# A block with a convolution and gated attention: the sigmoids of gates that are read back get a fixed place in ScalarE's queue

## The chip, the cores and the metric

The kernel runs on one core of a Trainium2 chip. The metric is the device time of one execution in microseconds (us); what is compared is the median of several runs. A profile of one execution is there too, with its own time. PE is TensorE (matmuls; PEld is its weight load), DVE is VectorE, ACT is ScalarE, POOL is GpSimd, SP is SyncE, which here only issues DMAs. Each engine works through a queue of its own in order; semaphores hold an instruction until what it needs is there.

## The reference, cut to what matters

For one sequence of 512 tokens of width 1024, the block is a half-weighted SwiGLU, a mixer, a second half-weighted SwiGLU and a norm. The change lies in the mixer:

```python
z = h @ w_in
cb, cc, cu, q, k, v, g_lr, r, ga, gb = jnp.split(z, SPLIT_POINTS, axis=-1)
y_conv = (cb * causal_short_conv(cc * cu, conv_w)) @ w_out_conv
...                                   # o: gated linear attention of q, k, v, g_lr, 4 heads
o = o * lax.rsqrt(jnp.mean(o * o, axis=-1, keepdims=True) + EPS)
y_gla = (o * gla_norm_g * jax.nn.silu(r)) @ w_out_gla
merged = jax.nn.sigmoid(ga) * y_conv + jax.nn.sigmoid(gb) * y_gla
return merged @ w_o
```

`ga` and `gb` are two gates of 512 x 1024. Each multiplies one product.

## The kernel before, in words

All arithmetic is float32, made from a rounded part and a rest: a weight tile `f` (128x1024) is cast on ACT to a high part `wh` (L309), and DVE subtracts to get the low part `wl` (L310). Three matmuls stand for one: high by high, high by low, low by high. There are three buffers each of `wh` and `wl`, so the cast of a step waits until PE is through with the step three places back. Weight tiles are loaded by SP (L283, ten buffers `f`) in the order of a list `STEPS`; `W.take` hands out the next pair and issues casts two steps ahead.

Most products are done as sets of seven products on half matrices (named m1, p2, q6, p5, q7, p4, p3, all run by `Set.run`, whose matmuls are L501, 24 of 256 columns in a step). Sums of weight tiles for them are made by accumulating DMAs from POOL (L287, `f<-f`) and on DVE (L296). Sums of results go through `tp` tiles (six buffers in the mixer); L506 copies a bank to one. Between the steps, hooks of `run_sets` place the parts of the attention: for head 3, `output(3)` (L1150 to L1159) and then `squares(3)`, in which ACT casts the sums of squares (L388), DVE subtracts (L389), PE sums over partitions with a matrix of ones (L1165 for the high part, L1166 for the low) and DVE turns the result (L1167).

The raw gates are made early, among the sets of `w_in`, and are stored in DRAM by ACT's queue (L1324, `ga<-tp` and `gb<-tp`), since there is no room for them. After the sets of `w_in` (the last are those of `r`, with a Silu on ACT, L1317) comes the product with `w_out_conv`: eight output blocks `d` of 128 rows, each one weight tile and 24 matmuls of 512 columns (`mm_single`, lines L337, L338, L339). Block `d` is multiplied by the sigmoid of block `d` of `ga`. In the same loop half a block of `gb` is read for later, into tiles that are free by then: the four `v` tiles for d below 4, the tiles `g` (E, M, KS, EX) after that. The product with `w_out_gla` follows as two sets of seven, with the operands cast in L549 and subtracted in L550.

A helper `gate` reads a block back by SP and applies the sigmoid on ACT, in place:

```python
t = T() if t is None else t
nc.sync.dma_start(t, gates_d[name][d])          # L1368; L1370 for a half block of two
nc.scalar.activation(t, t, AF.Sigmoid)          # L1372
```

The order of each engine's queue isn't the order of the source: a scheduler places each instruction in its engine's queue by what it expects to be ready. So an instruction that stands late in the source can come early in a queue. ACT functions come in tables; where the next function is in another table, an ACT_TABLE_LOAD stands in the queue.

Of the kernel before, what the change touches and what calls it, by code (L numbers as in the profile page):

```python
# [11 lines left out]
AF = mybir.ActivationFunctionType  # L12
# [6 lines left out]
KD = D // P  # L19
# [47 lines left out]
def unit_cols(u):  # L67
    return u[2] * len(u[3]) * u[4]
# [115 lines left out]
def block_kernel(ctx: ExitStack, tc: tile.TileContext, xT, vecs, gf, gup, wgl, wts, out):  # L184
    nc = tc.nc
# [20 lines left out]
    def tile_of(pool, shape, dtype=F32):  # L206
        cnt[0] += 1
        return pools[pool].tile(shape, dtype, tag=pool, name=f"{pool}{cnt[0]}")

    def T(dtype=F32):  # L210
        return tile_of("tp", [P, S], dtype)
# [31 lines left out]
    class Weights:  # L243
# [45 lines left out]
        def issue(self):  # L289
            at = self.issued  # L290
            self.fetch(at)
            for n in self.loads.get(at, ()):
                self.raw[n] = [self.dma(n + i) for i in range(4)] + [tile_of("f", [P, 1024])]
            for n in self.sums.get(at, ()):
                a11, a12, a21, a22, s3 = self.raw[n]
                nc.vector.tensor_tensor(out=s3, in0=a11, in1=a21, op=ALU.add)  # L296
                self.add(a21, a22)
            n, p = STEPS[at]
            w = unit_cols(PLAN[n])
            if p is None:  # L300
                raw = self.raw[n]
            else:
                a11, a12, a21, a22, s3 = self.raw[n]
                raw = {"m1": a11, "p2": a12, "q6": a11, "p5": a21, "q7": s3, "p4": a22,
                       "p3": a12}[p]
            late = at >= len(STEPS) - TAIL or ENDS[0] - TAIL <= at < ENDS[0] - 2
            h = tile_of("op" if late else "wh", [P, 1024], F32R)
            l = tile_of("op" if late else "wl", [P, 1024], F32R)
            nc.scalar.copy(h[:, :w], raw[:, :w])  # L309
            nc.vector.tensor_tensor(out=l[:, :w], in0=raw[:, :w], in1=h[:, :w].bitcast(F32),  # L310
                                    op=ALU.subtract)
            if p == "m1":
                self.add(a11, a21)
            if p == "p2":
                self.add(a12, a11)
            self.issued += 1
            self.ready.append((h, l))
# [10 lines left out]
    W = Weights(2)  # L328
# [12 lines left out]
    def mm_single(mat, kt, col, ah, al):  # L341
        o = MM()
        for u in single(mat, kt, col):
            h, l = W.take(u)
            for i in range(u[2]):
                k = u[1] + i
                mm3(o, h[:, i * P : (i + 1) * P], l[:, i * P : (i + 1) * P],
                    ah[k], al[k], k == 0, k == kt - 1)
        return o
# [124 lines left out]
    def mul(out_, a, b, eng=None):  # L474
        (eng or nc.vector).tensor_tensor(out=out_, in0=a, in1=b, op=ALU.mult)
# [449 lines left out]
    def mixer(norm, nxt):  # L925
# [301 lines left out]
        def pair(t):  # L1227
            return t.rearrange("p (e t) -> p e t", t=HW)

        def half(l):  # L1230
            return slice(l * HW, (l + 1) * HW)
# [128 lines left out]
        def parts(v):  # L1360
            r = [hl for i in v for hl in split_pair(i)]
            return [a for a, _ in r], [b for _, b in r]

        def gate(name, d, l=None, t=None):

            t = T() if t is None else t
            if l is None:
                nc.sync.dma_start(t, gates_d[name][d])  # L1368
            else:
                nc.sync.dma_start(pair(t), gates_d[name][d : d + 2, :, half(l)].rearrange(  # L1370
                    "e p t -> p e t"))
            nc.scalar.activation(t, t, AF.Sigmoid)  # L1372
            return t

        c_h, c_l = parts([Y[i][:, :, 2:] for i in range(4)])
        m = [two(d // 2)[:, d % 2] for d in range(KD)]
# [7 lines left out]
        AT = {3: "m1", 4: "p2", 6: "p5"}  # L1384
        gb = {}

        def early_gate(i, a, l, t):
            gb[i, a, l] = gate("gb", 4 * i + 2 * a, l, t)

        for d in range(KD):  # L1390
            t = gate("ga", d)
            yp = mm_single("w_out_conv", KD, d * P, c_h, c_l)
            mul(m[d], yp, t)
            if d < HEADS:
                tr, orow = (E, M) if d % 2 else (KS, QS)
                nc.vector.tensor_copy(
                    tr.rearrange("p (b c) -> p b c", c=32),
                    r64[:, 16 * d : 16 * (d + 1)].unsqueeze(2).to_broadcast([P, 16, 32]))
                nc.vector.transpose(orow, tr)
                mul(O[d], O[d], orow.unsqueeze(1).to_broadcast([P, 2, S]))  # L1400
            if d in AT:
                oo.make(AT[d])
            if d < 4:
                early_gate(0, d % 2, d // 2, vt[1][d])
            else:
                early_gate(1, d % 2, (d - 4) // 2, (E, M, KS, EX)[d - 4])
        oo.sum("q6")
        m_h, m_l = [None] * KD, [None] * KD

        def gla_done(i):  # L1410
# [56 lines left out]
    with phase("small2", f=10, tp=6, v=4, qk=2, g=1, y=4, small=1):  # L1467
        W.phase(4, 5)
        n2 = Norm(V_G2)
        mixer(nm, n2)  # L1470
# [46 lines left out]
```

## Time and profile before

| | |
|---|---|
| runs | 1196.65, 1197.68, 1200.97 us; median 1197.68 |
| profiled execution | 1196.36 us, of which the span from the first to the last instruction is 1194.6 us; 1.76 us lie around it |
| PE | 1179.0 us busy, 99% of the span |
| DVE, ACT, POOL | 74%, 53%, 10% |
| granted TensorE clock, mean | 0.995 |

In the profile, a time in the first column is that of the start of an instruction, counted from the start of the span; the second is how long it took. `L1372` is line 1372 of the kernel. In square brackets stands how long the engine was idle before the instruction, and what released it. "ACTq" and "SPq" are DMA issues and waits in an engine's queue, which aren't counted as busy. Numbers in buffer names are left out in the profile, and shown in the order of the queues below.

### The profile page before, as it was taken

The numbers are of one execution on the slowest core, as the hardware profiler recorded it, in microseconds if no ns is written. First come the engines' busy times: TensorE is split into PE (matmuls) and PEld (weight loads), VectorE is DVE, ScalarE is ACT, GpSimd is POOL, SyncE is SP. The second block draws the span as 40 slices with busy tenths as digits, with TensorE's granted clock in tenths as the row PEclk, the third lists the DMA queues.
The fourth block names the chain that finished last, engine by engine and source line by source line (L and its number), as shares of the span: only waits on it lengthen the run. The fifth ranks groups of instructions, "written<-read, shape, count | busy, mean of one in ns | idle before, by whom it ended". The sixth has DMA issues, their size and how long they took to land. (4 is left out here: it accounts for less than half of the span.)

```text
span 1194.6 us, 19198 instructions
## 1 busy us (share of the span) xinstructions
PE 1179.0 (99%) x7818; PEld 1086.8 (91%) x7818; DVE 878.7 (74%) x1044; ACT 630.3 (53%) x780; POOL 116.3 (10%) x155
## 2 busy tenths in 40 slices
PE   9999999999999999999989999999999999999997
PEld 8899999988888889999989998998889999998876
DVE  7976666897578765768668778676598665679955
ACT  6564444676245465646545467444346454556543
POOL 0011111111010000101001100200001111101100
PEclk9999999999999999999989999999999999999999
DMA  9477777678532326767867767552528777757721
GB/s 348 85 207 188 179 184 187 157 196 202 194 115 80 94 65 160 218 161 179 221 165 181 189 177 221 160 158 71 185 64 210 177 192 170 184 154 187 175 86 71
DMA packets 61224, 197.10 MB, mean 165 GB/s; under 512 B 6768, under 2 KB 13040, under 8 KB 61136
## 3 DMA queue, kind: packets, MB, share of 16 engines
q0 software_dynamic: 18560, 67.12, 30.6%
q1 hardware_dynamic: 37936, 124.27, 29.7%
q10 hardware_dynamic: 4640, 4.49, 1.2%
q8 instruction: 61, 1.00, 0.3%
q14 instruction: 27, 0.22, 0.1%
HBM read 124.55 MB, written 8.39 MB: 111 GB/s over the span
## 5 line engine op out<-in xcount | busy, mean ns | idle before, releaser
L501 PE MATMUL mm<-op,wh 128*128 128x256 f32 x3584 | 649.8, 284 | 1.5 <-ACT tp L506 1.5
L309 ACT CAST wh<-f 128x1024 fp32r<-128x1024 f32 (+1 forms) x335 | 350.2, 1047 | 436.7 <-PE mm L501 226.0
L501 PEld LDWEIGHTS mm<-op,wh 128*128 128x128 f32 x3584 | 560.4, 192 | 2.6 <-ACT tp L506 1.7
L310 DVE TENSOR_TENSOR wl<-f,wh 128x1024 fp32r<-128x1024 f32 (+1 forms) x335 | 406.9, 1217 | 179.9 <-ACT wh L309 174.9
L501 PE MATMUL mm<-op,wl 128*128 128x256 f32 x1792 | 508.1, 284 | 0.2 <-DVE wl L310 0.2
L501 PEld LDWEIGHTS mm<-op,wl 128*128 128x128 f32 x1792 | 344.1, 192 | 0.6 <-DVE wl L310 0.4
L287 POOL DMA_DIRECT2D f<-f x120 | 103.5, 865 | 927.0 <-DVE wl L310 506.1
L339 PE MATMUL mm<-op,wl 128*128 128x512 f32 x192 | 75.0, 391 | 0.5 <-DVE wl L310 0.5
L337 PE MATMUL mm<-op,wh 128*128 128x512 f32 x192 | 75.2, 392 | 0.2 <-ACT wh L309 0.2
L338 PE MATMUL mm<-op,wh 128*128 128x512 f32 x192 | 74.7, 389 | 0.0
L361 PE MATMUL mm<-op,wh 128*128 128x512 f32 x256 | 64.0, 392 | 0.0
L791 PE MATMUL mm<-wl,op 128*128 128x512 f32 x160 | 62.4, 390 | 0.7 <-DVE wl L310 0.7
L789 PE MATMUL mm<-wh,op 128*128 128x512 f32 x160 | 62.3, 389 | 0.0
L793 PE MATMUL mm<-wh,op 128*128 128x512 f32 x160 | 62.3, 389 | 0.0
L361 PEld LDWEIGHTS mm<-op,wh 128*128 128x128 f32 x256 | 48.0, 189 | 10.2
L506 ACT COPY tp<-mm 128x512 f32<-128x512 f32 x96 | 55.6, 580 | 1.0 <-DVE tp L1299 1.0
L296 DVE TENSOR_TENSOR f<-f,f 128x1024 f32<-128x1024 f32 x40 | 48.9, 1221 | 0.8
L339 PEld LDWEIGHTS mm<-op,wl 128*128 128x128 f32 x192 | 36.0, 188 | 8.4 <-DVE wl L310 1.0
L337 PEld LDWEIGHTS mm<-op,wh 128*128 128x128 f32 x192 | 36.0, 188 | 7.7 <-ACT wh L309 0.4
L338 PEld LDWEIGHTS mm<-op,wh 128*128 128x128 f32 x192 | 36.1, 188 | 7.4
L791 PEld LDWEIGHTS mm<-wl,op 128*128 128x128 f32 x160 | 30.1, 188 | 7.4 <-DVE wl L310 1.3
L793 PEld LDWEIGHTS mm<-wh,op 128*128 128x128 f32 x160 | 30.0, 188 | 6.2
(282 smaller groups left out, 1333.8 us busy)
## 6 DMA issues: line engine op xcount, KB each, us to landing
f<-wts SPq DMA_DIRECT2D x219, 512.0 KB, 4.4
f<-f POOLq DMA_DIRECT2D x120, 512.0 KB, 5.0
X<-xT SPq DMA_DIRECT2D x8, 256.0 KB, 5.2
xs<-X POOLq DMA_DIRECT2D x8, 256.0 KB, 2.3
ga<-tp ACTq DMA_DIRECT2D x8, 256.0 KB, 2.9
gb<-tp ACTq DMA_DIRECT2D x8, 256.0 KB, 3.3
tp<-ga SPq DMA_DIRECT2D x8, 256.0 KB, 5.3
X<-xs POOLq DMA_DIRECT2D x8, 256.0 KB, 6.3
```

The lines of the kernel that those rows point to most:

```text
L287: nc.gpsimd.dma_start(out_, a, accum_op=ALU.add)
L309: nc.scalar.copy(h[:, :w], raw[:, :w])
L310: nc.vector.tensor_tensor(out=l[:, :w], in0=raw[:, :w], in1=h[:, :w].bitcast(F32), op=ALU.subtract)
L337: nc.tensor.matmul(o, wh, ah, start=first, stop=False)
L338: nc.tensor.matmul(o, wh, al, start=False, stop=False)
L339: nc.tensor.matmul(o, wl, ah, start=False, stop=last)
L361: nc.tensor.matmul(o[c], w[:, s : s + P], a[k], start=k == 0 and j == 0, stop=k == kt - 1 and j == 2)
L501: nc.tensor.matmul(to, ww[:, s], aa[:, t], start=fresh and k == 0 and e == 0 and j == 0, stop=k == 3 and j == 2, skip_group_check=True)
L506: nc.scalar.copy(v, o)
L789: nc.tensor.matmul(o[t], bh[:, s], wh, start=fresh and k == 0, stop=False, skip_group_check=True)
L791: nc.tensor.matmul(o[t], bh[:, s], wl, start=False, stop=False, skip_group_check=True)
L793: nc.tensor.matmul(o[t], bl[:, s], wh, start=False, stop=k == 3, skip_group_check=True)
```

## The change

The sigmoid leaves `gate` and becomes a function of its own, which is traced at the loop of `w_out_conv`. An `issue_after` puts it in ACT's queue behind the weight cast that stands last in the source at that place (`W.cast`). The first two blocks of `ga` are read before the loop, and block d + 2 at step d. The half blocks of `gb` are read where they were in the source; their sigmoids come one loop step later, the last one behind the loop.

```diff
-            nc.scalar.copy(h[:, :w], raw[:, :w])
+            self.cast = nc.scalar.copy(h[:, :w], raw[:, :w]).ins
...
-            nc.scalar.activation(t, t, AF.Sigmoid)
             return t
+
+        def sigmoid(t):
+
+            with tc.issue_after(W.cast):
+                nc.scalar.activation(t, t, AF.Sigmoid)
...
+        ga = [gate("ga", d) for d in range(2)]
+        gb_new = []
+
         def early_gate(i, a, l, t):
             gb[i, a, l] = gate("gb", 4 * i + 2 * a, l, t)
+            gb_new.append(gb[i, a, l])

         for d in range(KD):
-            t = gate("ga", d)
+            t = ga[d]
+            if d + 2 < KD:
+                ga.append(gate("ga", d + 2))
+            sigmoid(t)
+            for g in gb_new:
+                sigmoid(g)
+            gb_new.clear()
             yp = mm_single("w_out_conv", KD, d * P, c_h, c_l)
             mul(m[d], yp, t)
...
         oo.sum("q6")
+        sigmoid(gb_new.pop())
```

What this does to the queues is seen in their order. First, ACT at the end of `output(3)`, in the middle of the sets of `w_in`. `wh` are weight casts, `v` and `g_564` are half blocks of `gb`, `tp_5963` is the high part that L1165 on PE needs, and the DMA stores a piece of the raw gate `gb`. Before:

```order
L1158 ACTIVATE g_563_3763<-aux_5888 128x512
L1372 ACT_TABLE_LOAD
L1372 ACTIVATE g_564_3764<-g_564_3764 128x512
L309 CAST wh_5932<-f_5519 128x1024
L1372 ACTIVATE v_3486<-v_3486 128x512
L1372 ACTIVATE v_3487<-v_3487 128x512
L1372 ACTIVATE v_3488<-v_3488 128x512
L1372 ACTIVATE v_3489<-v_3489 128x512
L388 CAST tp_5963<-g_561_3761 128x512
L1324 DMA gb<-tp_5960 128x2x256
L309 CAST wh_5972<-f_5523 128x1024
```

With the change:

```order
L1158 ACTIVATE g_563_3763<-aux_5888 128x512
L309 CAST wh_5932<-f_5519 128x1024
L309 CAST wh_5972<-f_5523 128x1024
L1324 DMA gb<-tp_5960 128x2x256
L388 CAST tp_5963<-g_561_3761 128x512
L309 CAST wh_6003<-f_5773 128x1024
```

Five sigmoids and a table load have left this place. L388 stands now behind one weight cast more, `wh_5972`, and behind the store. On PE, in the same place, L1165 stood behind ten matmuls of the step that uses `wh_5902`; it stands behind twenty now, and L1166 behind all 24:

```order
L501 MATMUL mm_5815<-op_4289,wh_5902 128x256
L1165 MATMUL aux_5967<-tp_5963,ones_r 128x512
L501 MATMUL mm_5815<-op_4288,wl_5903 128x256
L501 MATMUL mm_5815<-op_4288,wh_5902 128x256
L501 MATMUL mm_5815<-op_4289,wh_5902 128x256
L501 MATMUL mm_5815<-op_4288,wl_5903 128x256
L1166 MATMUL aux_5967<-tp_5964,ones_r 128x512
L501 MATMUL mm_6002<-op_4221,wh_5932 128x256
```

So both matmuls of the ones moved ten and more places back.

The second place is ACT at the end of the last set of `r` and in the first blocks of `w_out_conv`. `wh_7220`, `wh_7253`, `wh_7326` are the casts for blocks 0, 1 and 2. Before:

```order
L1372 ACT_TABLE_LOAD
L1372 ACTIVATE g_561_3761<-g_561_3761 128x512
L506 COPY tp_7178<-mm_6991 128x512
L309 CAST wh_7186<-f_6731 128x1024
L1356 CAST op_7298<-y_3483 128x1024
L1317 ACT_TABLE_LOAD
L1317 ACTIVATE tp_7180<-tp_7180 128x512
L1317 ACTIVATE tp_7215<-tp_7215 128x512
L309 CAST wh_7220<-f_7116 128x1024
L1311 ACTIVATE tp_7249<-mm_6991 128x512
L309 CAST wh_7253<-f_7148 128x1024
```

With the change (`wh_7330` is block 2, `wh_7370` block 3; `tp_7311` and `tp_7313` are blocks 0 and 1 of `ga`):

```order
L506 COPY tp_7178<-mm_6991 128x512
L309 CAST wh_7186<-f_6731 128x1024
L1356 CAST op_7298<-y_3483 128x1024
L1317 ACTIVATE tp_7180<-tp_7180 128x512
L309 CAST wh_7220<-f_7116 128x1024
L1317 ACTIVATE tp_7215<-tp_7215 128x512
L309 CAST wh_7253<-f_7148 128x1024
L1311 ACTIVATE tp_7249<-mm_6991 128x512
```

and, six rows further on (two table loads are among them),

```order
L1377 ACT_TABLE_LOAD
L1377 ACTIVATE tp_7311<-tp_7311 128x512
L1377 ACTIVATE tp_7313<-tp_7313 128x512
L309 CAST wh_7370<-f_7218 128x1024
L1377 ACTIVATE tp_7315<-tp_7315 128x512
L1377 ACTIVATE v_3487<-v_3487 128x512
L549 CAST op_7521<-O 128x1024
L309 CAST wh_7410<-f_7251 128x1024
```

The cast of block 0 moved ahead of the second Silu, and a sigmoid and two table loads ahead of it are gone. From block 3 on, a weight cast stands behind the sigmoid of a block read back, as it did before. On SP the reads of `ga` have moved a little too. Before:

```order
L283 DMA f_7364<-wts 128x1024
L1368 DMA tp_7311<-ga 128x512
L1368 DMA tp_7360<-ga 128x512
L1368 DMA tp_7400<-ga 128x512
L283 DMA f_7404<-wts 128x1024
```

With the change:

```order
L283 DMA f_7368<-wts 128x1024
L283 DMA f_7408<-wts 128x1024
L1368 DMA tp_7311<-ga 128x512
L1368 DMA tp_7313<-ga 128x512
L1368 DMA tp_7315<-ga 128x512
```

The weight tile of the last block of `w_out_conv` goes out ahead of the first read now. The reads of `gb` into `v` tiles stay where they were in SP's queue. POOL's queue is the same, and after `w_out_conv` all queues are.

## The prediction, made before the changed kernel ran

> **What bounds the kernel now.** First the page: how long the span is, and who is busy.
>
> ```profile
> span 1194.6 us, 19198 instructions
> ## 1 busy us (share of the span) xinstructions
> PE 1179.0 (99%) x7818; PEld 1086.8 (91%) x7818; DVE 878.7 (74%) x1044; ACT 630.3 (53%) x780; POOL 116.3 (10%) x155
> ```
>
> PE is busy for 99%. So only what makes PE wait, or slows it, can be won, and a busy microsecond less on ACT is worth nothing by itself. The view of who waited for whom, on PE, names the waits (total us, times, longest); the first row comes from the stretch 585 to 625 us, the other three from 700 to 800 us:
>
> ```profile
> PE aux L1165 <- ACT tp L388: 4.3, 1, 4.3
> ```
> ```profile
> PE mm L501 <- ACT tp L506: 1.5, 1, 1.5
> PE mm L339 <- DVE wl L310: 0.5, 1, 0.5
> PE mm L337 <- ACT wh L309: 0.2, 1, 0.2
> ```
>
> One wait of 4.3 us is the longest by far. It ends with the cast L388 on ACT. The timeline of ACT (start, us, ..., idle before) shows what stood ahead of it:
>
> ```profile
> 591.89 1.28 ACT L1372 ACT_TABLE_LOAD   x1
> 593.19 0.63 ACT L1372 ACTIVATE g<-g 128x512 f32<-128x512 f32 x1
> 593.73 1.03 ACT L309 CAST wh<-f 128x1024 fp32r<-128x1024 f32 x1
> 595.96 0.63 ACT L1372 ACTIVATE v<-v 128x512 f32<-128x512 f32 x1 [1.19 <-DMA v<-gb]
> 597.87 0.63 ACT L1372 ACTIVATE v<-v 128x512 f32<-128x512 f32 x1 [1.28 <-DMA v<-gb]
> 600.01 1.30 ACT L1372 ACTIVATE v<-v 128x512 f32<-128x512 f32 x2 [1.51 <-DMA v<-gb]
> 600.77 0.37 ACTq L1324 DMA_DIRECT2D gb<-tp  x1
> 601.22 0.60 ACT L388 CAST tp<-g 128x512 fp32r<-128x512 f32 x1
> ```
>
> Five sigmoids of `gb`, whose results are not used before the product with `w_out_gla`, were placed here. Three times ACT stands still for a read, and L388 with all that follows stands behind. The timeline of PE in the same stretch:
>
> ```profile
> 596.86 0.28 PE L501 MATMUL mm<-op,wl 128*128 128x256 f32 x1
> 596.98 0.40 PE L501 MATMUL mm<-op,wh 128*128 128x256 f32 x2
> 597.22 0.28 PE L501 MATMUL mm<-op,wl 128*128 128x256 f32 x1
> 597.34 0.28 PE L501 MATMUL mm<-op,wh 128*128 128x256 f32 x1
> 601.87 0.79 PE L1165 MATMUL aux<-tp,ones_r 128*128 128x512 f32 x1 [4.26 <-ACT tp L388]
> 602.47 0.41 PE L501 MATMUL mm<-op,wh 128*128 128x256 f32 x1
> ...
> 606.52 0.48 PE L501 MATMUL mm<-op,wh 128*128 128x256 f32 x2
> ```
>
> Three matmuls start in 0.36 us before the wait (596.86 to 597.22), so 0.12 us each. After it they are slow until 606.52. The table by stretches (PE, PEld, DVE, ACT, POOL, then the granted clock, DMA share, GB/s) says why:
>
> ```profile
> 601.90:606.50 4.60, 4.60 (x19) 4.41 (x20) 2.55 (x4) 1.46 (x2) 0.00 (x0) 0.50 0.12 41
> ```
>
> The clock is granted at half after the pause. The wait costs its idle time and this.
>
> **First term: the stall at 597 us.** The change takes the sigmoids from this place. The next start was due at 597.34 + 0.12 = 597.46; full pace is back at 606.52, 9.06 us later. By the order of the queue, PE did 17 matmuls L501 (four between the two of ones, 13 behind) and L1165 and L1166 in that time. At full pace that is 17 x 0.12 = 2.04 us and, with 0.23 us for one of 512 columns (below), 0.46 us: 2.5 us. The stall costs 9.06 - 2.5 = **6.56 us**, of which 4.3 us are idle.
>
> What is late next? PE's step that holds L1165 began ten matmuls before 597.46, at 596.26; L1165 comes after twenty now, at 598.66, and L1166 at 598.66 + 0.23 + 4 x 0.12 = 599.37. On ACT, the cast `wh_5972` is released by the step that ended at 596.26, and takes 1.03 us: done at about 597.4. The store of `gb` behind it needs a sum on DVE that isn't early:
>
> ```profile
> 596.46 0.69 DVE L1302 TENSOR_TENSOR tp<-mm,tp 128x512 f32<-128x512 f32 x1 [0.44 <-PE mm L501]
> ```
>
> That ends at 597.15, so the issue (0.37) runs to 597.8, and L388 (0.60) to 598.4: 0.2 us ahead of L1165. On DVE the subtract for `wl_5973` stands ahead of L389 now; with 1.22 us (below) it ends at 598.7, and L389, as long as L1302, at 599.4. So L1166 comes at the same time as its operand, and PE may wait 0.1 us. Both ends: if a release costs a few tenths at each of these four handovers, up to 1 us of waiting; if the store should hold L388 to where it is now, all 6.56 us stay (a rival). I take 0.2 us. The five sigmoids themselves (5 x 0.63) land in the loop of `w_out_conv`.
>
> [...]
>
> **Second term: the start of `w_out_conv`.** PE's timeline there:
>
> ```profile
> 718.42 0.28 PE L501 MATMUL mm<-op,wl 128*128 128x256 f32 x1
> 718.85 0.50 PE L337 MATMUL mm<-op,wh 128*128 128x512 f32 x1 [0.15 <-ACT wh L309]
> 719.19 0.40 PE L338 MATMUL mm<-op,wh 128*128 128x512 f32 x1
> 720.11 0.50 PE L339 MATMUL mm<-op,wl 128*128 128x512 f32 x1 [0.53 <-DVE wl L310]
> 720.45 0.40 PE L337 MATMUL mm<-op,wh 128*128 128x512 f32 x1
> 720.68 0.39 PE L338 MATMUL mm<-op,wh 128*128 128x512 f32 x1
> ```
>
> The pace for 512 columns is 0.23 us (720.45 to 720.68). L337 was due at 718.54, the L338 of 720.68 four matmuls later at 719.46. So **1.2 us** are lost, more than the 0.7 us that the waits add up to. The cause is the cast of the first block's weights, late on ACT:
>
> ```profile
> 713.40 1.05 ACT L309 CAST wh<-f 128x1024 fp32r<-128x1024 f32 x1 [1.71 <-DMA f<-f]
> 714.35 1.04 ACT L1356 CAST op<-y 128x1024 fp32r<-128x1024 f32 x1
> 715.41 1.28 ACT L1317 ACT_TABLE_LOAD   x1
> 716.71 1.16 ACT L1317 ACTIVATE tp<-tp 128x512 f32<-128x512 f32 x2
> 717.77 1.03 ACT L309 CAST wh<-f 128x1024 fp32r<-128x1024 f32 x1
> ```
>
> A table load stands between, because the queue has a sigmoid of `gb` among the Silus. With the change the cast at 713.40 still waits for its accumulating DMA, but the table load is gone, and one Silu instead of two is ahead of the next weight cast: it starts at 715.4 + 0.6 = 716.0, 1.8 us sooner, is done at 717.1, and the subtract at about 718.3, just before PE is ready at 718.54.
>
> ```profile
> L310 DVE TENSOR_TENSOR wl<-f,wh 128x1024 fp32r<-128x1024 f32 (+1 forms) x335 | 406.9, 1217 | 179.9 <-ACT wh L309 174.9
> ```
>
> I take the whole 1.2 us; the bounds are none of it (if the subtract comes after another on DVE) and all.
>
> **What costs nothing while it is covered.** The sigmoids go among the eight blocks of `w_out_conv`. A block lasts 24 x 0.23 = 5.4 us of PE; ACT's work for one is a cast (1.03), two sigmoids (1.26) and now and then an operand cast (1.04), so 3.3 us. Block 3's matmuls begin at 718.54 + 3 x 5.4 = 734.9 us; its cast stands behind the reads of `ga` blocks 0 and 1:
>
> ```profile
> 720.46 1.37 SPq L1368 DMA_DIRECT2D tp<-ga  x3
> ```
> ```profile
> DMA to landing us min/median/max: 2.1/4.6/7.5
> ```
>
> SP issues these reads after one weight tile more, whose buffer is free when the subtract for block 1 is done, by the work ahead of it on DVE at about 721.3; so the reads go out at about 721.8, 1.3 us later than now. Landed at the longest 7.5 us later, sigmoid, cast and subtract end at 721.8 + 0.4 + 7.5 + 0.6 + 1.0 + 1.2 = 732.5: 2.4 us of cover is left. Without it each us late is one on PE. The 1.5 us wait at L506, near 798 us, hangs on an accumulating DMA of the last set of `w_out_gla`; nothing ahead of it changes order, so I leave it (bounds: gone, or 1 us longer). DMAs, the arithmetic and the bytes are the same.
>
> **Sum.** 6.56 - 0.2 + 1.2 = 7.6 us off the profiled execution: a span of 1187.0 us, a time of 1188.8 us. The median of the runs stands 1.3 us above the profiled one (1197.68 against 1196.36), so **1190.1 us**. A difference of 0.5% (6.0 us) is about the least that a measurement of this kernel tells from no change: 1191.7 us is that limit, and the forecast is only 1.6 us beyond it.
>
> **Rivals.**
>
> *The stall stays, behind the store.* L388 now stands behind the store of `gb`, which left at 600.77 in the row above. There it stood behind L388 in the queue and went out while the last sigmoid ran, and its sum was ready at 597.15: so it was late by the sigmoids alone, which speaks against this rival. For it speaks that no row shows it in its new place. If it leaves no sooner, L388 ends at 601.8 as before and only 1.2 us are won: 1196.5 us. If it's held half as long, about 1193.
>
> *The cover in `w_out_conv` is thinner than it looks.* Two operand casts wait there for sums on DVE, and a weight cast stands behind each. If the second term isn't won and one wait of a us or two, short enough to leave the clock, comes in: -6.4 + 1 to 2, so 1192.3 to 1193.3 us.
>
> *Slower: a weight cast caught behind a late read.* Behind the sigmoid of a block stands the cast of a later block's weights. It decides when a read takes 9.9 us from issue to landing (7.5 + 2.4), where 7.5 is the longest seen; then PE waits, and after a pause like that at 597 us it runs at half clock. Priced as two such stalls (2 x 6.56 = 13.1 us): -7.6 + 13.1 = +5.5, 1203.2 us. Against it: before, sigmoids stood ahead of the same casts, and ACT waited for reads of `ga` for 1.0 us in all (700 to 770 us):
>
> ```profile
> ACT tp L1372 <- DMA tp<-ga: 1.0, 3, 0.4
> ```
>
> *It doesn't do what it says.* The queues show the sigmoids moved, so only a stall that other work causes at the same place could keep the time: 1197.7 us.
>
> **How the numbers follow.** The forecast 0.64, with its own range 1188 to 1192 us; the store 0.13; thinner cover 0.15; slower 0.05; nothing 0.03. The forecast lies beyond the limit for nine parts in ten (0.58), thinner cover for a fifth (0.03): faster 0.61. The store, the rest of those two and nothing at all are within 0.5%: 0.34. Slower: 0.05. The range goes from 1187.5 (without the L506 wait 1188.6, and less where the new median stands nearer to its fastest runs) to 1196.5 us, the store's case; above it lie the slower case and nothing, below it little.
>
> **What would show it.** First term: PE's wait L1165 <- L388 is gone or under 0.5 us, and the granted clock is 1.00 from 597 to 607 us. A wait of L1165 that remains with the store's issue late on ACT would show the first rival. Second term: no table load between the Silus of `r` at the end, and PE passes from L501 to L337 without a wait. Cover: no wait of L337 on L309 between 725 and 765 us. The prediction is wrong if the whole shift isn't there by 725 us, or if PE has a new wait between 725 and 800 us.

## The result, and the profile after

| | before | with the change |
|---|---|---|
| runs beside each other | 1196.65 to 1200.97 us, 4 runs | 1188.07 to 1192.07 us, 4 runs |
| median | 1198.13 us | 1190.39 us |
| profiled execution | 1196.36 us, span 1194.6 | 1192.07 us, span 1190.4 |
| mean granted clock | 0.995 | 0.997 |

The ratio is 0.9934, with a 95% interval of 0.9915 to 0.9954: the change makes the kernel 7.7 us faster. The forecast was 1190.1 us, so 7.6 us less than the 1197.68 shown then. But the two profiled spans differ by 4.2 us only; the profiled execution of the change is the slowest of its four runs. The comparison of the traces has to find where 7.6 us were won and, in this one execution, some 3.4 lost again.

The head of the page of the change:

```profile
span 1190.4 us, 19195 instructions
PE 1177.9 (99%) x7818; PEld 1085.6 (91%) x7818; DVE 878.5 (74%) x1044; ACT 625.5 (53%) x777; POOL 116.3 (10%) x155
```

Three instructions less, all on ACT: three table loads. They are 3 x 1.28 = 3.8 us less of work on an engine that is busy for 53%, and no measure of the gain. What PE waits for tells more (total us, times, longest; the three longest):

```profile
PE mm L501 <- ACT tp L506: 2.8, 1, 2.8
PE aux L228 <- POOL ones L225: 1.1, 1, 1.1
PE mm L791 <- DVE wl L310: 0.8, 1, 0.8
```

The wait of 4.3 us at L1165 is gone, and so are those at L337 and L339. The wait at L506 grew from 1.5 to 2.8 us. Each of the three places in turn.

**First place.** ACT and PE, in their timelines, where the stall was (start, us, what, in brackets the idle time before it):

```profile
596.36 1.05 ACT L309 CAST wh<-f 128x1024 fp32r<-128x1024 f32 x1 [1.83 <-PE mm L501]
597.20 0.37 ACTq L1324 DMA_DIRECT2D gb<-tp  x1
597.61 0.62 ACT L388 CAST tp<-g 128x512 fp32r<-128x512 f32 x1 [0.21 <-issue]
```
```profile
598.67 0.40 PE L1165 MATMUL aux<-tp,ones_r 128*128 128x512 f32 x1
...
599.38 0.44 PE L1166 MATMUL aux<-tp,ones_r 128*128 128x512 f32 x1
```

The cast L388 ends at 598.2 and L1165 starts at 598.67 with no idle time; L1166 follows without one too. The table by stretches (PE, PEld, DVE, ACT, POOL busy, the granted clock, DMA share, GB/s) has full clock over the whole place, and in its second row over the loop of `w_out_conv`:

```profile
597.30:606.50 9.20, 9.20 (x77) 9.11 (x77) 7.15 (x13) 5.83 (x9) 0.86 (x1) 1.00 0.86 251
715.00:755.00 40.00, 40.00 (x178) 33.14 (x177) 30.71 (x32) 24.33 (x32) 3.44 (x4) 1.00 0.63 176
```

**Second place.** ACT at the end of the sets of `r`, and PE as it enters `w_out_conv`:

```profile
708.05 1.04 ACT L1356 CAST op<-y 128x1024 fp32r<-128x1024 f32 x1
709.00 0.63 ACT L1317 ACTIVATE tp<-tp 128x512 f32<-128x512 f32 x1
709.54 1.03 ACT L309 CAST wh<-f 128x1024 fp32r<-128x1024 f32 x1
```
```profile
712.08 0.28 PE L501 MATMUL mm<-op,wl 128*128 128x256 f32 x1
712.20 0.40 PE L337 MATMUL mm<-op,wh 128*128 128x512 f32 x1
```

No table load, one Silu, then the first block's cast; L337 follows 0.12 us after the last L501, at full pace.

**How much that is.** Both executions come to L1311, a row ahead of the first place, at the same time. Some 165 us later POOL makes the same sum of weights in the first set of `w_out_gla`. Before, these two rows were:

```profile
588.45 0.59 ACT L1311 ACTIVATE tp<-mm 128x512 f32<-128x512 f32 x1
760.44 0.86 POOL L287 DMA_DIRECT2D f<-f  x1 [4.58 <-DVE wl L310]
```

With the change:

```profile
588.47 0.59 ACT L1311 ACTIVATE tp<-mm 128x512 f32<-128x512 f32 x1
752.89 0.86 POOL L287 DMA_DIRECT2D f<-f  x1 [4.58 <-DVE wl L310]
```

From row to row it is 760.44 - 588.45 = 171.99 us before and 752.89 - 588.47 = 164.42 us after: 7.57 us are won by there.

**Third place, where it is given back.** The chain of waits after that point, with the change:

```profile
767.07 9.21 DMA f<-f
...
776.38 1.06 ACT wh L309
...
786.86 4.77 DMA f<-f
...
792.68 0.59 ACT tp L506
793.26 0.04 issue
```

and before:

```profile
774.62 7.80 DMA f<-f
...
782.51 1.06 ACT wh L309
...
792.99 4.79 DMA f<-f
...
798.83 0.59 ACT tp L506
```

These are the last two sums of weight tiles by accumulating DMA, for the second set of `w_out_gla`. The first one took 9.21 us instead of 7.80. From its end on the chain is the same in both, step by step: the cast L309 starts 16.30 us before L506 in the one and 16.32 in the other. So L506 comes 1.4 us later against the work of PE, and PE waits 2.85 us instead of 1.5. PE's row, and the stretch behind the wait:

```profile
793.31 0.79 PE L501 MATMUL mm<-op,wh 128*128 128x256 f32 x2 [2.85 <-ACT tp L506]
```
```profile
793.30:796.60 3.30, 3.29 (x15) 3.29 (x16) 3.30 (x6) 0.90 (x1) 0.00 (x0) 0.50 0.46 137
```

Behind the longer wait stands a second cost, which the shorter one before did not have: 3.3 us at half clock. That is 1.3 us more of waiting and 3.3 / 2 = 1.7 us of slow work, 3.0 us of the 3.4 lost. The question for the experiments is whether the change does this, or whether it happens to either kernel.

### The profile page after: what moved, and what is told of

The parts are those of the page before. It is cut to its first block, busy times and chain, and to the rows that moved or that the text cites. A ratio compares the mean times of both kernels' runs of the same rounds, so it can differ in the third digit from the quotient of the medians.

```text
span 1190.4 us, 19195 instructions
## 1 busy us (share of the span) xinstructions
PE 1177.9 (99%) x7818; PEld 1085.6 (91%) x7818; DVE 878.5 (74%) x1044; ACT 625.5 (53%) x777; POOL 116.3 (10%) x155
## 5 line engine op out<-in xcount | busy, mean ns | idle before, releaser
L501 PE MATMUL mm<-op,wh 128*128 128x256 f32 x3584 | 649.6, 284 | 2.8 <-ACT tp L506 2.8
L309 ACT CAST wh<-f 128x1024 fp32r<-128x1024 f32 (+1 forms) x335 | 350.1, 1046 | 439.4 <-PE mm L501 227.2
L501 PEld LDWEIGHTS mm<-op,wh 128*128 128x128 f32 x3584 | 560.2, 192 | 4.0 <-ACT tp L506 3.0
L501 PE MATMUL mm<-op,wl 128*128 128x256 f32 x1792 | 508.1, 284 | 0.1
L501 PEld LDWEIGHTS mm<-op,wl 128*128 128x128 f32 x1792 | 344.0, 192 | 0.6 <-DVE wl L310 0.5
L337 PE MATMUL mm<-op,wh 128*128 128x512 f32 x192 | 75.1, 391 | 0.0
L339 PE MATMUL mm<-op,wl 128*128 128x512 f32 x192 | 74.9, 390 | 0.0
L506 ACT COPY tp<-mm 128x512 f32<-128x512 f32 x96 | 55.7, 580 | 1.9 <-DVE tp L1299 1.0
L339 PEld LDWEIGHTS mm<-op,wl 128*128 128x128 f32 x192 | 36.0, 188 | 7.5
L337 PEld LDWEIGHTS mm<-op,wh 128*128 128x128 f32 x192 | 36.1, 188 | 7.4
```

Source lines behind the costliest of these rows:

```text
L309: self.cast = nc.scalar.copy(h[:, :w], raw[:, :w]).ins
L337: nc.tensor.matmul(o, wh, ah, start=first, stop=False)
L339: nc.tensor.matmul(o, wl, ah, start=False, stop=last)
L501: nc.tensor.matmul(to, ww[:, s], aa[:, t], start=fresh and k == 0 and e == 0 and j == 0, stop=k == 3 and j == 2, skip_group_check=True)
L506: nc.scalar.copy(v, o)
```

## The experiments

The theory at the start: the gain is all of `gb`'s sigmoids, at the first two places, and the third place varies from one execution to the next. The rivals: that `ga`'s reads and pins have a part in it, and that the change itself lengthens the wait at L506.

### Each half of the change alone

`e1_gb_only` keeps the pinned sigmoids of `gb`, and does `ga` as before:

```diff
-        ga = [gate("ga", d) for d in range(2)]
...
-            t = ga[d]
-            if d + 2 < KD:
-                ga.append(gate("ga", d + 2))
-            sigmoid(t)
+            t = gate("ga", d)
+            nc.scalar.activation(t, t, AF.Sigmoid)
```

> Only the sigmoids of gb get the fixed place in ScalarE's queue; ga is read and its sigmoid is placed as before the change. Theory (the two terms of the prediction both come from sigmoids of gb, five at 592 to 601 us and one at 710 us): as fast as the whole change, 7 to 8 us below the kernel before, no wait of L1165 on L388, no table load between the last Silus of r. Rival (the read-ahead or the place of ga's sigmoids has a part in it): less than 6 us below, or a new wait of PE between 725 and 765 us.

Measured: 1191.17 us median, beside 1199.67 of the kernel before; ratio 0.9938 (0.9920 to 0.9955). The wait at L1165 is gone and PE has none in `w_out_conv`, as expected; its only one from 580 to 800 us is 3.3 us at L506.

`e2_ga_only` does the opposite. It keeps `ga`'s reads ahead and its pinned sigmoids, and `gb`'s sigmoids are traced behind their reads again:

```diff
         def early_gate(i, a, l, t):
             gb[i, a, l] = gate("gb", 4 * i + 2 * a, l, t)
-            gb_new.append(gb[i, a, l])
+            nc.scalar.activation(gb[i, a, l], gb[i, a, l], AF.Sigmoid)
```

> Only ga is read two tiles ahead and gets its sigmoids behind the weight casts; the sigmoids of gb are placed as before. Theory: nothing is won; PE waits 4.3 us at L1165 on L388 with half a clock behind it, and loses 1.2 us at the start of w_out_conv, as before; within 1 us of the kernel before. Rival (ga matters): 2 us or more below it.

Measured: 1198.69 us; ratio 0.9993 (0.9982 to 1.0003). PE's waits in it, from the view of who waited for whom:

```profile
PE aux L1165 <- ACT tp L388: 4.3, 1, 4.3
PE mm L501 <- ACT tp L506: 3.0, 1, 3.0
PE mm L339 <- DVE wl L310: 0.5, 1, 0.5
```

The stall at L1165 and the wait at L339 are those of the kernel before, to a tenth. With `e1_gb_only` as fast as the whole change, the gain comes from `gb`. And the wait at L506 is 3.0 us here, without the pins of `gb` and without any gain ahead of it: a long wait at the third place does not need the change.

### The change with nothing else, a second time

`e3_change_again` is the change itself, for its spread.

> The change once more, as the partner of the others. Its first profile had gained 7.6 us by 755 us, and lost 3.4 us of it at the end of w_out_gla: PE waited 2.85 us for the copy L506 where it had waited 1.5, and had half a clock until 796.7 us. Theory: the place is a race of a sum by DMA against the eight reads of X and varies from run to run; so spans between 1186 and 1190 us, 7 to 10 us below the kernel before, by whether the clock drops there. Rival: the wait of 2.85 us is a fixed price of the new order of the reads, and comes again to within 0.2 us.

Measured: 1190.96 us, in runs from 1189.27 to 1193.72; ratio 0.9935 (0.9917 to 0.9953). Their spans go from 1187.6 to 1192.0 us, two of the six above the 1190 expected. The wait at L506 was 3.1 us in its profile, behind a sum of 9.4 us. By itself that says only that the wait isn't the same to 0.2 us. The sums and waits of all the profiles that share the order of this place say more. From the same views:

| kernel | first sum lands after | last sum lands after | wait at L506 | clock behind it |
|---|---|---|---|---|
| before | 7.8 us | 4.8 us | 1.5 us | full |
| `e5_before_busy_pe` (below) | 7.7 | 4.8 | 1.3 | full |
| `e7_no_read_ahead` (below) | 7.7 | 5.8 | 2.3 | full |
| change | 9.2 | 4.8 | 2.85 | half for 3.3 us |
| `e2_ga_only` | 9.4 | 4.8 | 3.0 | half |
| `e3_change_again` | 9.4 | 4.8 | 3.1 | half |
| `e1_gb_only` | 9.7 | 5.0 | 3.3 | half |

The first sum lands near 7.7 us or near 9.4, and both occur with the sigmoids of `gb` where they were and where they are now. In `e7_no_read_ahead` it is the last sum that took a us longer, and the wait with it.

### What makes the third place late

In both kernels POOL issues eight reads of the residual, 256 KB each, just ahead of the first sum. In the change's timeline of POOL:

```profile
759.85 4.31 POOL L1453 DMA_DIRECT2D X<-xs  x8 [6.09 <-DVE op L550]
767.07 0.89 POOL L287 DMA_DIRECT2D f<-f  x1 [2.92 <-DVE wl L310]
```

The sum takes 9.21 us beside them; the one at 786.86, in the chain above, 4.77. So the reads were suspected. `e4_reload_late` moves them behind the issue of the last sum:

```diff
-            nc.gpsimd.dma_start(out_, a, accum_op=ALU.add)
+            self.added = nc.gpsimd.dma_start(out_, a, accum_op=ALU.add).ins
...
-            for k in range(KD):
-                nc.gpsimd.dma_start(x[k], xs[k])
+            with tc.issue_after(W.added):
+                for k in range(KD):
+                    nc.gpsimd.dma_start(x[k], xs[k])
-        run_sets(lambda i: Set(oo, gla_done(i)), hooks={(0, "p3"): [reload]})
+        run_sets(lambda i: Set(oo, gla_done(i)), hooks={(1, "p2"): [reload]})
```

> The change, and the eight reads that bring X back (L1453 in the change) issued on POOL behind the last sum by DMA of w_out_gla instead of ahead of the last two. Theory (the sum f<-f at 767 us takes 9.2 us since the eight reads share its DMA engines, the weight cast behind it is late, and the chain ends in PE's wait at L506): that sum lands in about 5 us, PE's wait at L506 goes from 2.85 us to under 0.5, the granted clock stays at 1.00 from 785 to 800 us; 1.5 to 4.5 us below the change. Rival (the chain is set by the last sum itself, 4.8 us behind a subtract, and by DVE's work): the wait stays at 1.3 us or more, and the time within 1 us of the change.

Measured: 1189.23 us, in four runs that lie within 0.5 us; ratio 0.9919 (0.9903 to 0.9934). That is 1.7 us below `e3_change_again`, measured beside it, as the theory had it, and the clock stayed full. But the first sum took 6.9 us and not 5, and the wait at L506 was 1.5 us and not under 0.5. POOL's timeline shows where the reads went:

```profile
784.76 0.86 POOL L287 DMA_DIRECT2D f<-f  x1 [16.62 <-DVE wl L310]
785.29 4.11 POOL L1454 DMA_DIRECT2D X<-xs  x7
790.78 0.54 POOL L1454 DMA_DIRECT2D X<-xs  x1 [1.37 <-DMA f<-f]
```

The reads go out 0.5 us after the last sum, which lands after 5.7 us, 0.9 more than in most profiles. I took the reads for the cause; that isn't shown, since the last sum took 5.8 us in two profiles without a read beside it (`e7_no_read_ahead` and, below, `e6_before_reload_behind_cast`). `e8_reload_behind_cast` holds them until the weight cast behind that sum is done, by a copy of one column of it on POOL:

```diff
-            for k in range(KD):
-                nc.gpsimd.dma_start(x[k], xs[k])
+            seen = front.tile([P, 1], F32, tag="seen", name="seen")
+            cast = nc.gpsimd.tensor_copy(seen, W.ready[-1][0][:, 0:1].bitcast(F32)).ins
+            with tc.issue_after(cast):
+                for k in range(KD):
+                    nc.gpsimd.dma_start(x[k], xs[k])
-        run_sets(lambda i: Set(oo, gla_done(i)), hooks={(0, "p3"): [reload]})
+        run_sets(lambda i: Set(oo, gla_done(i)), hooks={(1, "p2"): [reload]})
```

> The change, and the eight reads that bring X back issued only when the last weight cast of w_out_gla is done. In the run with the reads behind the issue of the last sum, that sum still shared the DMA engines with them, and PE still waited 1.5 us at L506. Theory: without any read beside it the last sum lands in under 5 us, PE's wait at L506 is under 0.5 us, the clock stays at 1.00; about 1.3 us below that run, so a ratio to the kernel before of about 0.991. Rival (what is left of the wait is the sum's own length): the wait stays at 1 us or more. A cost that could eat it: X comes back some 6 us later, and the first additions to X behind w_o would wait for it.

Measured: 1188.65 us, beside 1198.06 of the kernel before on that chip; ratio 0.9929 (0.9916 to 0.9941), five runs from 1188.38 to 1189.82. PE's only wait from 580 to 800 us, and POOL:

```profile
PE mm L501 <- ACT tp L506: 0.4, 1, 0.4
```
```profile
786.16 0.86 POOL L287 DMA_DIRECT2D f<-f  x1 [16.46 <-DVE wl L310]
792.13 1.24 POOL L1453 COPY seen<-wh 128x1 f32<-128x1 f32 x1 [5.12 <-ACT wh L309]
793.32 4.31 POOL L1456 DMA_DIRECT2D X<-xs  x8
```

The first sum lands after 6.1 us, the last after 4.8, and the clock stays full. In the three versions with the reads moved (`e4_reload_late`, this one and `e6_before_reload_behind_cast` below) the first sum takes 6.0 to 6.9 us, against 7.7 to 9.7 in the table, no wait at L506 is above 1.5 us and no half clock follows. So the long wait of 2.85 us and more comes from the reads beside the first sum. What is left of it, 0.4 us here and 1.4 to 1.5 in the other two, goes with the last sum: 4.8 us here, 5.7 to 5.8 there.

The median is the lowest of all versions, but by the ratio it is not below `e4_reload_late` (0.9919, on another chip), so the 1.3 us that were expected over that version were not seen. Nor is its profiled span shorter (1188.1 against 1187.7 us), though PE's wait is 1.1 us shorter: this execution came to L1311, ahead of all three places, 1.55 us later (590.47 against 588.92 us).

### The same mending on the kernel before

If the third place belongs to both kernels, mending it in both must leave the gain of the first two places. `e6_before_reload_behind_cast` is the kernel before with the edit of `e8_reload_behind_cast`.

> The kernel before, and the eight reads that bring X back issued on POOL only when the last weight cast of w_out_gla is done (a copy of one column of that cast's result holds them). Theory (the place at the end of w_out_gla is independent of the change and costs 1.5 us of wait in a good run, 3 us and a half clock in a bad one): PE's wait at L506 under 0.5 us, 1.5 to 5 us below the kernel before, and a narrower spread of its times; the stall at L1165 is there as before. Rival: the place is bound by the sums themselves, nothing is won.

Measured: 1195.30 us; ratio to the kernel before 0.9982 (0.9974 to 0.9991). The wait at L506 came to 1.4 us, not under 0.5, and the clock stayed full there. The last sum took 5.8 us, where that of `e8_reload_behind_cast` took 4.8, and this 1.0 us is the difference between the two waits; a weight cast ahead of it hangs on a load in both (1.8 us of waiting here). Why the last sum takes the one or the other stays open. From this kernel to `e8_reload_behind_cast`, on the same chip, it is 1195.30 - 1188.65 = 6.65 us between the medians. Its stretch from L1311 to the sum on POOL, where the third place has no part, is 171.12 us, and that of `e8_reload_behind_cast` 164.19: 6.93 us. What the mending brings is also much the same in both: the median falls by 2.8 us from the kernel before to this one and by 3.3 from `e7_no_read_ahead` to `e8_reload_behind_cast`, and the granted clock, as the mean of the runs, rises by 0.001 in both pairs (0.9958 to 0.9969 and 0.9975 to 0.9986). So both kernels lose there, as far as these runs tell about alike. The stall itself looks so (PE's timeline; the rows between are slow too):

```profile
601.79 0.79 PE L1165 MATMUL aux<-tp,ones_r 128*128 128x512 f32 x1 [3.96 <-ACT tp L388]
...
605.14 0.45 PE L501 MATMUL mm<-op,wh 128*128 128x256 f32 x2
605.43 0.28 PE L501 MATMUL mm<-op,wl 128*128 128x256 f32 x1
605.55 0.40 PE L501 MATMUL mm<-op,wh 128*128 128x256 f32 x2
```

PE is slow from 601.79 to 605.14, 3.35 us, where the profile of before had 4.6. So the stall costs between 5.6 (3.96 + 3.35 / 2) and 6.6 us from execution to execution. The granted clock in the two traces shows where this comes from: here it is 1.00 up to 601.60 us and 0.61 over the 4.40 us from there to 606.00, so half for 3.4 us; in the profile of before it is half from 599.9 to 606.7, for 6.8 us. There it fell while PE still waited, as the clock of 0.76 over that wait shows:

```profile
597.60:601.86 4.26, 0.02 (x1) 0.00 (x0) 0.01 (x1) 2.43 (x5) 0.00 (x0) 0.76 0.58 215
```

### Is the half clock a part of the price of the stall?

`e5_before_busy_pe` leaves the stall in the kernel before as it is, and gives PE 24 matmuls to do in it, whose result is overwritten:

```diff
             st = AUX()
+            if h == 3:
+                busy = xo.get("m1")[0][:, :S]
+                for _ in range(24):
+                    nc.tensor.matmul(st, ones_r, busy, start=True, stop=True)
             nc.tensor.matmul(st, ones_r, sh, start=True, stop=False)
```

> The kernel before, with 24 matmuls of 512 columns more on PE ahead of L1165 of the last head (their result is overwritten, so it isn't used). They are ready at once and last about 24 x 0.23 = 5.5 us, so PE works while ACT is still held up by the sigmoids of gb. The two matmuls of ones stand at the start of their step here, so PE waits there for DVE's L389, to about 602.6 us. Theory (the half clock behind the stall comes of PE's idle time, and is 2.3 us of the 6.56): with under 1.5 us of idle time the clock stays at 1.00 from 602 to 607 us, and three matmuls of 256 columns take 0.36 us there. Rival (the clock falls for something else at this place): 0.50 there, and 0.64 us for three. The time as before to within 2 us, either way.

Measured, in a single execution: 1195.09 us, span 1193.4. PE's timeline:

```profile
596.18 5.76 PE L1168 MATMUL aux<-op,ones_r 128*128 128x512 f32 x24
601.78 0.40 PE L1169 MATMUL aux<-tp,ones_r 128*128 128x512 f32 x1
602.41 0.50 PE L1170 MATMUL aux<-tp,ones_r 128*128 128x512 f32 x1 [0.23 <-DVE tp L389]
602.75 0.40 PE L501 MATMUL mm<-op,wh 128*128 128x256 f32 x2
602.99 0.28 PE L501 MATMUL mm<-op,wl 128*128 128x256 f32 x1
603.11 0.40 PE L501 MATMUL mm<-op,wh 128*128 128x256 f32 x2
```

L388 is as late as before (it ends at 601.63) and the matmul of ones still starts at 601.8, now straight behind the 24 others. But the three L501 behind it take 0.36 us (602.75 to 603.11): full pace at once, and the granted clock from 601.9 to 606.5 us is 1.00, where the profile of before had 0.50. So the slow stretch follows from PE being idle here: 4.26 us there, 0.23 us in this run. A single execution doesn't fix the gain in time to less than the spread of this kernel, and no more is read from it.

### Is reading ahead needed?

`e7_no_read_ahead` is the change with its pins, but each block of `ga` read at its own step:

```diff
-        ga = [gate("ga", d) for d in range(2)]
...
-            t = ga[d]
-            if d + 2 < KD:
-                ga.append(gate("ga", d + 2))
+            t = gate("ga", d)
             sigmoid(t)
```

> The change without the reads two tiles ahead: each block of ga is read at its own loop step, all sigmoids stand behind the casts. Theory (the scheduler puts the reads early anyway, the read-ahead does nothing for the time): as the change, ratio to the kernel before 0.992 to 0.995, PE has no wait between 720 and 765 us. Rival (without it a weight cast is caught behind a read): a wait of PE at L337 or L339 there, and 1 us or more above the change.

Measured: 1191.93 us; ratio 0.9951 (0.9935 to 0.9967), at the edge of what was expected, in an interval that overlaps the change's. PE has no wait from 720 to 765 us, and its stretch from L1311 to the sum on POOL is 164.18 us, the same as with the reads ahead in `e3_change_again` (164.18). So reading ahead isn't what the gain hangs on. The median is 1 us above that of `e3_change_again`, by the ratios 2 us, which is less than these runs tell apart.

## Why the prediction was right

**The sum and the time.** 1190.39 us against 1190.1 forecast, and 7.57 us won in the profiled execution by the sum on POOL against 7.6. That this agrees so well has some luck in it. The profiled span was forecast at 1187.0 us and came at 1190.4, because of the third place; the median agrees since the 1.3 us by which the median of before stands above its profile were added, and the new profile stands above its own median instead. And other executions of the kernel before lose 0.9 us less at the stall (171.12 us from row to row in `e2_ga_only` and `e6_before_reload_behind_cast`, against 171.99), where the clock was at half for 3.4 us and not for 6.8. The gain of the first two places is 6.9 to 7.6 us; the medians give 7.7 (5.5 to 10.2 by the interval).

**First term, the stall (6.56 us, less 0.2).** Right, and in its steps. L1165 was forecast at 598.66 and L1166 at 599.37; they started at 598.67 and 599.38. L388 ended 0.2 us sooner than forecast, since the issue of the store began (597.20) before the weight cast was through (596.36 + 1.05 = 597.41), and the 0.1 to 0.2 us of waiting that I allowed did not occur there (PE lost 0.24 us at 709.5 us instead, which `e3_change_again` did not). For the half clock after the pause I set the measured 4.6 us into the sum. That is what one execution showed, and it isn't fixed: the clock was at half for 3.4 us in `e2_ga_only` and `e6_before_reload_behind_cast`, and for 6.8 us in the profile of before, of which the 4.6 us are the part behind the wait. Against the two with the shorter stretch the versions with the change gain 171.12 - 164.18 = 6.94 us by the sum on POOL, where it was 7.57 against the profile of before.

**Second term, the start of `w_out_conv` (1.2 us).** Right: from the last L501 to the sixth matmul of the product PE took 2.49 us before and 1.29 with the change. The first block's cast, by the prediction at 716.0 less the 6.4 us already won, so 709.6, started at 709.54, and PE passed into the product with no wait.

**The cover in `w_out_conv`.** Held, with more room than forecast. The reads of `ga` and block 3's cast and subtract, from SP's, ACT's and DVE's timelines:

```profile
715.11 2.33 SPq L1368 DMA_DIRECT2D tp<-ga  x5
```
```profile
721.67 0.63 ACT L1377 ACTIVATE tp<-tp 128x512 f32<-128x512 f32 x1 [1.41 <-DMA tp<-ga]
722.21 1.04 ACT L309 CAST wh<-f 128x1024 fp32r<-128x1024 f32 x1
```
```profile
723.29 1.22 DVE L310 TENSOR_TENSOR wl<-f,wh 128x1024 fp32r<-128x1024 f32 x1
```

The subtract ends at 724.5. PE needs it at 712.20 + 3 x 5.4 = 728.4, so 3.9 us were left where 2.4 were forecast. The reads went out when they should (715.11, against 721.8 less the 6.4 us), but the two that stand ahead of this cast had landed 6.6 us later, and I had counted 0.4 for the issue and the longest landing, 7.5.

**The wait at L506, left as it was (bounds: gone, or 1 us longer).** This is the step that was too narrow. That nothing ahead of it changes order is true, and the long wait doesn't need the change. But I took one execution's 1.5 us for the kernel's. It grew by 1.35 us, past the bound of 1, and with it came half clock, for which the prediction had no term. Over the profiles with the reads in their old place the wait is 1.3 to 3.3 us, and the four waits of 2.85 us and more came with half clock for 3.3 to 3.4 us each, so that in the profiled execution 3 us of the gain were gone. It did not spoil the forecast because such executions occur with `gb`'s sigmoids at their old place too (`e2_ga_only`): the profile of before was a good execution at that place, the change's a bad one. With the reads out of the way in `e8_reload_behind_cast` the range of the runs is 1.4 us, where the change had 4.0 and, the second time, 4.5.

**The rivals.** The stall behind the store: the store left at 597.20, 3.6 us sooner than before, with the sigmoids gone, and the reason given against this rival was the right one. The thinner cover, and the cast caught behind a late read: no wait of PE from 585 to 786 us. Nothing moves: no.

## What to carry to other kernels

An engine that is busy for half the time (here ACT, 53%) can still set the end, by one instruction that stands in its queue behind others which wait for a DMA and whose results nobody needs yet: look at what ended PE's longest wait, then at what stood ahead of it in that engine's own timeline. Price such a stall as its idle time and the slow stretch behind it, as the profile shows them (here 4.3 and 2.3 us), and leave out the busy time of what is moved. And before a place is taken as fixed because its order doesn't change, see whether it hangs on a transfer beside others: such a place can vary (here PE waited 1.3 to 3.3 us), and one profile of each kernel can then show a difference, here 3 us, that the change hasn't made.

## What the runs showed of the hardware

The granted clock, in the ten profiles, at the two waits looked at. At L506 it was at half with waits of PE of 2.85 us (the change), 3.0 (`e2_ga_only`), 3.1 (`e3_change_again`) and 3.3 us (`e1_gb_only`), and stayed full with 0.4 (`e8_reload_behind_cast`), 1.3 (`e5_before_busy_pe`), 1.4 (`e6_before_reload_behind_cast`), 1.5 (before and `e4_reload_late`) and 2.3 us (`e7_no_read_ahead`). At L1165 it was at half with waits of 3.96 (`e6_before_reload_behind_cast`), 4.26 (before) and 4.31 us (`e2_ga_only`). Whether the length of the wait alone decides it these profiles don't tell, and none has a wait between 2.3 and 2.85 us. It was at half for 3.4 us in the change, for 3.3 in `e1_gb_only` and `e3_change_again` (0.89 over 15 us), for 3.4 at both places of `e2_ga_only` (0.83 over 10 us at L506), for 3.4 in `e6_before_reload_behind_cast`, and for 6.8 us in the profile of before. Why it was the longer time there, with a wait no longer than that of `e2_ga_only`, was not settled. With PE kept busy through the wait at L1165 (`e5_before_busy_pe`, one execution) it was 1.00 from 601.9 to 606.5 us.

Ten profiles have the two accumulating DMAs of 512 KB. The last one landed in 4.8 to 5.0 us in seven, and in 5.7 to 5.8 in three: one with the eight reads of 256 KB issued 0.5 us behind it, two without. The first one landed in 6.0 to 6.9 us in three profiles without these reads ahead of it in POOL's queue, and in 7.7 to 7.8 (three) or 9.2 to 9.7 us (four) with them. Why it was the one or the other of the last two was not settled.
